# Low parts of twelve weight blocks made by accumulating transfers, in half of the value buffers

## The chip, the cores and the metric

The kernel runs on one core of a Trainium2 chip, as one program in one launch. TensorE (PE) multiplies, VectorE (DVE) and ScalarE (ACT) do elementwise work, GpSimd (POOL) has almost nothing to do here but to issue some transfers, and SyncE (SP) issues all the others. The metric is device time in microseconds (us); before the change the median of three runs is 876.96 us (876.62 to 877.98).

## The reference

One decoder layer over 512 positions of width 1024, all in float32:

```
h      = rms_norm(x)*(1+scale1)+shift1                    # scale, shift, gates: silu(c) @ w_ada
xr, gr, q, k, v, gm = split(h @ w_in)
y_rnn  = rg_lru(causal_conv(xr)) * gelu(gr)               # gated linear recurrence, 8 blocks of 128
y_attn = rms_norm(softmax(q1 k1)v - lam*softmax(q2 k2)v)  # 8 heads, two maps each, causal, rotary q, k
merged = sigmoid(gm0)*(y_rnn @ w_proj_rnn) + sigmoid(gm1)*(y_attn @ w_proj_attn)
x      = x + gate1*(merged @ w_out)
out    = x + gate2*(relu(h2 @ w_ff1)**2 @ w_ff2),  h2 = rms_norm(x)*(1+scale2)+shift2
```

## The kernel before

All large products keep float32 accuracy from a faster format: each operand is split into a high part, rounded to the matmul's format (`fp32r`), and a low part, the rest. A product is then three matmuls (`mm3`, lines 127 to 131): high by high, high by low and low by high.

Weights come in blocks of 128x1024, numbered in the order of their use (w0, w1, ...). `load_w` (lines 113 to 125) loads a block from HBM into one of three buffers (`w`, issued by SP), ScalarE rounds it to the high part `wh` (L122), and VectorE subtracts to get the low part `wl` (L123); `wh` and `wl` have two buffers each. A block feeds 24 matmuls: `project` makes one block of 128 output channels, `token_major` needs four blocks for the 512 columns of a quarter of q and k (`qk_quarter`) or of half of the values (`v_half`).

Around the change the program goes like this. After the recurrence's input and the first quarter of q and k, `v_half(0)` runs beside the recurrence's gates (`gates(n)`, n from 0 to 7): each gate takes two products of 128 channels (pg0_n, pg1_n) with small weights wgh and wgl, which live in halves (index 0 for blocks 0 to 3, index 1 for blocks 4 to 7), and ScalarE makes r, ig and th of them. Then come the attention heads, and between their steps the rest of the work is filled in by a written order, `PLAN`: gN is the gate projection gmN, sN the recurrence of block N (a product, a scan and a product on VectorE, L461, L462 and L471, and the split L473), qN a quarter of q and k, tN its transposes, v1 the second half of the values, pN the recurrence's output projection. Within that a scheduler sets the order of each engine ahead of time; each engine then works through its own list strictly in order and waits where a semaphore asks for it. A part under `tc.high_priority(n)` is drawn forward by it.

One step of a head (`softmax_step`, `weights_t`, `value_step`): TensorE makes two score banks (sc, L582), VectorE masks them and takes the maximum (L587), ScalarE makes the exponentials e (L589), VectorE joins the two maps (rr, cc and e, L593 to L596), TensorE transposes e (aT, L604), ScalarE or VectorE copies it (aTs, L607 and L609), TensorE multiplies it with the values (po, L615).

PSUM has four banks called mm (for projections), two called sc (for scores and also for pg), and single ones. The pool `v` has eight SBUF buffers of 128x512. They hold the eight halves of the gate weights (wgh, wgl), and later the four tiles of each half of the values (vs0_0 to vs0_3, vs1_0 to vs1_3), which ScalarE copies out of the mm banks (L505).

Of the kernel before, what the change touches and what calls it, by code (L numbers as in the profile page):

```python
# [17 lines left out]
F32R = mybir.dt.float32r  # L18
BF16 = mybir.dt.bfloat16
I32 = mybir.dt.int32  # L20
AF = mybir.ActivationFunctionType
ALU = mybir.AluOpType
# [18 lines left out]
QT0 = 1  # L41
ADA = (2, 4)
HP = 130
TABLES = 4
DV0, DV1 = (0,), (0,)
NWARM, NWARM2 = 2, 1
# [7 lines left out]
def build(tc, out, x, xT_in, c, pos, vecs, reps, ada, w_xr, w_xr7, w_qk, w_v, w_gr, w_gm, w_lru,  # L54
# [4 lines left out]
    with ExitStack() as es:  # L59
# [6 lines left out]
        mix_es = ExitStack()  # L66
        mix = mix_es.enter_context(tc.tile_pool(name="mix", bufs=1))

        B_Q, B_Y, B_M, B_H, B_V, B_T, B_A, B_R = 12, 24, 8, 16, 8, 4, 6, 5

        def slot(tag, bufs, name, dt=F32):
            return (big if tag in "mh" else mix).tile([P, S], dt, name=name, tag=tag, bufs=bufs)
# [35 lines left out]
        def f32(t):  # L108
            return t.bitcast(F32)

        n_unit = [0]
        last_wh = [None]

        def load_w(src, n=1024):
            u = n_unit[0]
            n_unit[0] += 1
            w = wpool.tile([P, 1024], F32, name=f"w{u}", tag="w", bufs=3)
            nc.sync.dma_start(w[:, :n], src)
            wh = wpool.tile([P, 1024], F32R, name=f"wh{u}", tag="wh", bufs=2)
            wl = wpool.tile([P, 1024], F32R, name=f"wl{u}", tag="wl", bufs=2)  # L120
            with tc.high_priority(HP):
                i_w = nc.scalar.copy(wh[:, :n], w[:, :n])  # L122
                nc.vector.tensor_tensor(wl[:, :n], w[:, :n], f32(wh)[:, :n], op=ALU.subtract)  # L123
            last_wh[0] = i_w
            return wh, wl
# [4 lines left out]
            nc.tensor.matmul(ps, lh, rl, start=False, stop=False, skip_group_check=more)  # L130
            nc.tensor.matmul(ps, ll, rh, start=False, stop=last, skip_group_check=more)  # L131

        def project(src, act, name):

            wh, wl = load_w(src)
            ps = bank(name)
            for k in range(KC):
                c0 = slice(k * P, (k + 1) * P)
                mm3(ps, wh[:, c0], wl[:, c0], act[k][0], act[k][1], k == 0, k == KC - 1)
            return ps  # L140
# [266 lines left out]
        def lru_weights():  # L407
            wg = []
            for j in range(2):
                w = wpool.tile([P, 1024], F32, name=f"wg{j}", tag="w", bufs=3)  # L410
                nc.sync.dma_start(w, w_lru[j])
                halves = []
                for i in range(2):
                    wh = slot("v", B_V, f"wgh{j}_{i}", F32R)
                    wl = slot("v", B_V, f"wgl{j}_{i}", F32R)
                    nc.scalar.copy(wh, w[:, i * S:(i + 1) * S])
                    split_l(wl, w[:, i * S:(i + 1) * S], wh)
                    halves.append((wh, wl))
                wg.append(halves)
            return wg  # L420
# [62 lines left out]
                except StopIteration as e:  # L483
                    return e.value

        def token_major(srcs, name):
            pss = [bank(f"{name}{t}") for t in range(TB)]
            for u in range(4):
                wh, wl = load_w(srcs[u])
                for t in range(TB):  # L490
                    tc0 = slice(t * P, (t + 1) * P)
                    for k2 in range(2):
                        k = 2 * u + k2
                        c0 = slice(k2 * S, (k2 + 1) * S)
                        mm3(pss[t], h[k][0][:, tc0], h[k][1][:, tc0], wh[:, c0], wl[:, c0],
                            k == 0, k == KC - 1)
                yield
            return pss

        def v_half(hf):  # L500
            pss = yield from token_major(w_v[hf], f"v{hf}_")
            vs = []
            for t in range(TB):
                v = slot("v", B_V, f"vs{hf}_{t}")
                nc.scalar.copy(v, pss[t])  # L505
                vs.append(v)
            return vs

        def qk_quarter(qt):

            pss = yield from token_major(w_qk[qt], f"qk{qt}_")
            s2 = tiny(f"qs{qt}", 32)
            rot = []
            v4 = lambda t: t.rearrange("p (m g d) -> p m g d", m=2, g=4)
# [166 lines left out]
        yr = []  # L681

        def gate(n, th):
            ps = project(w_gm[n], h, f"gm{n}")
            nc.scalar.activation(th, ps, AF.Tanh, scale=0.5)
            return th

# [450 lines left out]
```

## Time and profile before

| | |
|---|---|
| median of the runs | 876.96 us |
| the profiled execution | 876.41 us, its span 874.6 us |
| TensorE busy | 861.0 us (98%), granted clock 1.00 |
| VectorE busy | 651.5 us (74%) |
| ScalarE busy | 449.2 us (51%) |
| POOL busy | 15.1 us (2%) |
| weight blocks split by L122 and L123 | 113 |
| bytes read from HBM | 113.51 MB |

The busy time of TensorE counts a matmul from its start to its end, and matmuls overlap, so 98% doesn't say that nothing is lost; the time from the start of one matmul to the start of the next shows it. A row of the timeline gives start, duration, engine, line and operation, and in brackets how long the engine was idle before and what ended it.

### The profile page before, as it was taken

The numbers are of one execution on the slowest core, as the hardware profiler recorded it, in microseconds if no ns is written. First come the engines' busy times: TensorE is split into PE (matmuls) and PEld (weight loads), VectorE is DVE, ScalarE is ACT, GpSimd is POOL, SyncE is SP. The second block draws the span as 40 slices with busy tenths as digits, with TensorE's granted clock in tenths as the row PEclk, the third lists the DMA queues.
The fourth block names the chain that finished last, engine by engine and source line by source line (L and its number), as shares of the span: only waits on it lengthen the run. The fifth ranks groups of instructions, "written<-read, shape, count | busy, mean of one in ns | idle before, by whom it ended". The sixth has DMA issues, their size and how long they took to land.

```text
span 874.6 us, 11292 instructions
## 1 busy us (share of the span) xinstructions
PE 861.0 (98%) x4012; PEld 705.5 (81%) x4012; DVE 651.5 (74%) x1251; ACT 449.2 (51%) x748; POOL 15.1 (2%) x50
## 2 busy tenths in 40 slices
PE   6999999999999999999999999999999999999998
PEld 3888887877878888888888888888888888888887
DVE  6997995599859855786758556858766885876397
ACT  6673547985536543535623343747545544554461
POOL 1000000000000000000000000000000000002110
PEclk9999999999999999999999999999999999999999
DMA  8979425412255372238336332822641344139572
GB/s 315 370 250 319 152 97 134 136 68 73 87 131 169 99 191 76 93 87 227 110 126 210 132 121 75 273 87 72 193 148 70 128 161 169 49 126 235 120 122 96
DMA packets 64572, 128.92 MB, mean 147 GB/s; under 512 B 6146, under 2 KB 30850, under 8 KB 64516
## 3 DMA queue, kind: packets, MB, share of 16 engines
q1 hardware_dynamic: 59236, 122.97, 43.3%
q0 software_dynamic: 5280, 5.24, 3.9%
q8 instruction: 31, 0.51, 0.2%
q14 instruction: 25, 0.20, 0.1%
HBM read 113.51 MB, written 2.10 MB: 132 GB/s over the span
## 4 chain that ended last, share of the span: by engine, by line
PE 86%; DVE 10%; DMA 1%; issue 1%; ACT 1%; SPq 1%; ACTq 0%; DVEq 0%
PE f L131 6%; PE f L129 6%; PE f L130 6%; PE X L131 3%; PE X L130 3%; PE X L129 3%; PE gm L129 3%; PE gm L130 3%; PE gm L131 3%; DVE wl L123 2%; PE sc L582 2%; PE qk L131 2%; PE qk L129 2%; PE qk L130 2%; PE xr L129 2%; PE pr L129 2%
## 5 line engine op out<-in xcount | busy, mean ns | idle before, releaser
L122 ACT CAST wh<-w 128x1024 fp32r<-128x1024 f32 (+1 forms) x113 | 118.0, 1044 | 214.5 <-issue 48.1
L123 DVE TENSOR_TENSOR wl<-w,wh 128x1024 fp32r<-128x1024 f32 (+1 forms) x113 | 137.0, 1213 | 68.1 <-ACT wh L122 64.5
L131 PE MATMUL f<-h2h,wl 128*128 128x512 f32 x240 | 93.5, 390 | 0.4 <-DVE wl L123 0.4
L130 PE MATMUL f<-h2l,wh 128*128 128x512 f32 x240 | 93.2, 389 | 0.0
L129 PE MATMUL f<-h2h,wh 128*128 128x512 f32 x240 | 92.9, 390 | 0.0
L131 PEld LDWEIGHTS f<-h2h,wl 128*128 128x128 f32 x240 | 45.0, 188 | 10.1 <-DVE wl L123 0.8
L130 PEld LDWEIGHTS f<-h2l,wh 128*128 128x128 f32 x240 | 45.1, 188 | 9.4
L129 PEld LDWEIGHTS f<-h2h,wh 128*128 128x128 f32 x240 | 45.0, 188 | 9.3
L130 PE MATMUL gm<-hl,wh 128*128 128x512 f32 x128 | 51.0, 398 | 0.0
L129 PE MATMUL qk<-wh,hh 128*128 128x512 f32 x128 | 50.7, 396 | 0.0
L129 PE MATMUL gm<-hh,wh 128*128 128x512 f32 x128 | 50.5, 394 | 0.0
L131 PE MATMUL gm<-hh,wl 128*128 128x512 f32 x128 | 50.5, 394 | 0.0
L131 PE MATMUL qk<-wh,hl 128*128 128x512 f32 x128 | 50.4, 394 | 0.0
L130 PE MATMUL qk<-wl,hh 128*128 128x512 f32 x128 | 50.4, 394 | 0.0
L941 DVE TENSOR_TENSOR p_1l<-b,p_1h 128x1024 fp32r<-128x1024 f32 x24 | 29.4, 1223 | 26.3 <-ACT p_1h L940 26.1
L589 ACT ACTIVATE e<-e,nm 128x128 f32<-128x128 f32 (+3 forms) x64 | 35.7, 559 | 24.4 <-DVE nm L587 24.4
L940 ACT CAST p_1h<-b 128x1024 fp32r<-128x1024 f32 x24 | 25.2, 1051 | 31.0 <-PE f L130 22.9
L941 DVE TENSOR_TENSOR p_0l<-b,p_0h 128x1024 fp32r<-128x1024 f32 x24 | 29.3, 1223 | 15.0 <-ACT p_0h L940 13.8
L587 DVE CUSTOM_DVE_ANT_0 e<-sc,mask 128x128 f32<-128x128 f32 (+3 forms) x64 | 30.3, 484 | 9.9 <-PE sc L582 9.9
L940 ACT CAST p_0h<-b 128x1024 fp32r<-128x1024 f32 x24 | 25.3, 1055 | 24.2 <-PE X L131 12.4
L188 DVE CUSTOM_DVE_ANT_0 ada<-ada,cb,bada 128x1024 f32<-128x1024 f32 x16 | 20.5, 1283 | 14.3 <-DMA ada<-in_ada 14.1
L984 DVE TENSOR_TENSOR b<-b,b 128x1024 f32<-128x1024 f32 x24 | 29.1, 1220 | 0.1
(444 smaller groups left out, 2216.9 us busy)
## 6 DMA issues: line engine op xcount, KB each, us to landing
ada<-in_ada SPq DMA_DIRECT2D x64, 256.0 KB, 5.8
w<-in_w_ff SPq DMA_DIRECT2D x32, 512.0 KB, 3.2
b<-in_w_ff SPq DMA_DIRECT2D x30, 512.0 KB, 3.4
w<-in_w_qk SPq DMA_DIRECT2D x16, 512.0 KB, 3.2
w<-in_w_gm SPq DMA_DIRECT2D x16, 512.0 KB, 3.7
ada<-in_ada SPq DMA_DIRECT2D x16, 512.0 KB, 3.3
b_t<-in_w_ff POOLq DMA_DIRECT2D x10, 512.0 KB, 6.5
w<-in_w_gr SPq DMA_DIRECT2D x8, 512.0 KB, 4.0
```

Source lines behind the costliest of these rows:

```text
L122: i_w = nc.scalar.copy(wh[:, :n], w[:, :n])
L123: nc.vector.tensor_tensor(wl[:, :n], w[:, :n], f32(wh)[:, :n], op=ALU.subtract)
L129: nc.tensor.matmul(ps, lh, rh, start=first, stop=False, skip_group_check=more)
L130: nc.tensor.matmul(ps, lh, rl, start=False, stop=False, skip_group_check=more)
L131: nc.tensor.matmul(ps, ll, rh, start=False, stop=last, skip_group_check=more)
L188: nc.vector.tensor_tensor_reduce(w, w, cb, 1.0, bada[:, col:col + 1], op0=ALU.mult, op1=ALU.add, accum_out=mod[:, col:col + 1])
L582: nc.tensor.matmul(ps[m][:, :nn], q[m][:, qc], k[m][r][:, :nn], start=r == 0, stop=r == 1)
L587: nc.vector.tensor_tensor_reduce(e[:, :n], ps[m][:, :n], mask[:, S - n:], 1.0, 1e30, op0=ALU.add, op1=ALU.min, accum_out=nm)
L589: nc.scalar.activation(e[:, :n], e[:, :n], AF.Exp, bias=nm, scale=-1.0, accum_out=sums[:, m:m + 1])
L940: nc.scalar.copy(v4(wh), v)
L941: nc.vector.tensor_tensor(v4(wl), v, f32(v4(wh)), op=ALU.subtract)
L984: nc.vector.tensor_tensor(d, d, s_, op=ALU.add)
```

## The change

`load_w` gets a second way, `by_dma`, for twelve blocks: the gate projections gm2 to gm5 (blocks w27, w28, w33, w34) and the second and third quarter of q and k (w29 to w32, w35 to w38). There ScalarE writes, for each half of the block, the negated and rounded weight into a buffer, and GpSimd issues a transfer that reads the same half of the weight from HBM once more and adds it to the buffer: weight minus its high part. VectorE's subtraction falls away. The buffers for it are four of the eight `v` buffers, now called `u`; the other four stay `v`. The gate weights' halves with index 0 live in `u`, those with index 1 in `v`; the first half of the values is in `v`, the second in `u`. The negated copy is drawn forward by 260, the rounding copy by 130 as before. `Pair` lets the two halves be addressed as one tile.

```diff
+HP_DMA = 260
+DMA_G, DMA_Q = (2, 3, 4, 5), (1, 2)
-        B_Q, B_Y, B_M, B_H, B_V, B_T, B_A, B_R = 12, 24, 8, 16, 8, 4, 6, 5
+        B_Q, B_Y, B_M, B_H, B_V, B_T, B_A, B_R = 12, 24, 8, 16, 4, 4, 6, 5
...
+            if by_dma:
+                lows = []
+                with tc.high_priority(HP_DMA):
+                    for i in range(2):
+                        cols = slice(i * S, (i + 1) * S)
+                        wl = slot("u", B_V, f"wl{u}_{i}", F32R)
+                        nc.scalar.activation(wl, w[:, cols], AF.Copy, scale=-1.0)
+                        nc.gpsimd.dma_start(wl, src[:, cols].bitcast(F32R), accum_op=ALU.add)
+                        lows.append(wl)
+                wh = wpool.tile([P, 1024], F32R, name=f"wh{u}", tag="wh", bufs=2)
+                with tc.high_priority(HP):
+                    last_wh[0] = nc.scalar.copy(wh, w)
+                return wh, Pair(lows)
...
-                    wh = slot("v", B_V, f"wgh{j}_{i}", F32R)
-                    wl = slot("v", B_V, f"wgl{j}_{i}", F32R)
+                    wh = slot("v" if i else "u", B_V, f"wgh{j}_{i}", F32R)
+                    wl = slot("v" if i else "u", B_V, f"wgl{j}_{i}", F32R)
...
-                v = slot("v", B_V, f"vs{hf}_{t}")
+                v = slot("u" if hf else "v", B_V, f"vs{hf}_{t}")
...
-            pss = yield from token_major(w_qk[qt], f"qk{qt}_")
+            pss = yield from token_major(w_qk[qt], f"qk{qt}_", qt in DMA_Q)
...
-            ps = project(w_gm[n], h, f"gm{n}")
+            ps = project(w_gm[n], h, f"gm{n}", n in DMA_G)
```

The scheduler orders all engines anew with this. ScalarE at the end of the recurrence's gates, before (the last number of a name counts the buffers; pg0_7 and pg1_7 are the last gate's products, v0_0 to v0_3 the banks of the values' first half):

```order
L505 COPY vs0_0_1725<-v0_0_1349 128x512
L436 CAST xch7_1706<-xc7_1337 128x512
L505 COPY vs0_1_1727<-v0_1_1350 128x512
L505 COPY vs0_2_1729<-v0_2_1351 128x512
L122 CAST wh26_1872<-w26_1870 128x1024
L444 ACTIVATE r6_1699<-pg0_6_1691,vec_93 128x512
L446 ACTIVATE ig6_1701<-pg1_6_1692,vec_93 128x512
L449 ACTIVATE th6_1704<-r6_1699,sp4_624 128x512
L444 ACTIVATE r7_1718<-pg0_7_1710,vec_93 128x512
L446 ACTIVATE ig7_1720<-pg1_7_1711,vec_93 128x512
L449 ACTIVATE th7_1723<-r7_1718,sp4_624 128x512
L505 COPY vs0_3_1731<-v0_3_1352 128x512
```

And ScalarE at the same place now:

```order
L148 CAST wh26_1872<-w26_1870 128x1024
L470 ACTIVATE r6_1699<-pg0_6_1691,vec_93 128x512
L472 ACTIVATE ig6_1701<-pg1_6_1692,vec_93 128x512
L475 ACTIVATE th6_1704<-r6_1699,sp4_624 128x512
L138 ACTIVATE wl27_0_1905<-w27_1903 128x512
L138 ACTIVATE wl27_1_1908<-w27_1903 128x512
L470 ACTIVATE r7_1718<-pg0_7_1710,vec_93 128x512
L138 ACTIVATE wl28_0_1970<-w28_1968 128x512
L138 ACTIVATE wl28_1_1973<-w28_1968 128x512
L472 ACTIVATE ig7_1720<-pg1_7_1711,vec_93 128x512
L475 ACTIVATE th7_1723<-r7_1718,sp4_624 128x512
L531 COPY vs0_0_1725<-v0_0_1349 128x512
```

Three copies of the values (vs0_0 to vs0_2) moved from ahead of the gates' last functions to behind them, and four negated copies (wl27, wl28) came in between.

TensorE at the same place, before (gm0 is the first gate projection, sc0_0_0 and sc0_0_1 the score banks of head 0's first step):

```order
L129 MATMUL gm0_1776<-hh0_195,wh25_1772 128x512
L130 MATMUL gm0_1776<-hl0_199,wh25_1772 128x512
L129 MATMUL pg0_7_1710<-xch7_1706,wgh0_1_760 128x512
L130 MATMUL pg0_7_1710<-xcl7_1708,wgh0_1_760 128x512
L131 MATMUL pg0_7_1710<-xch7_1706,wgl0_1_761 128x512
L129 MATMUL pg1_7_1711<-xch7_1706,wgh1_1_770 128x512
L130 MATMUL pg1_7_1711<-xcl7_1708,wgh1_1_770 128x512
L131 MATMUL pg1_7_1711<-xch7_1706,wgl1_1_771 128x512
L131 MATMUL gm0_1776<-hh0_195,wl25_1773 128x512
L129 MATMUL gm0_1776<-hh1_238,wh25_1772 128x512
L582 MATMUL sc0_0_0_1751<-kh0_2_0_1473,qs0_0_0_1458 128x256
L582 MATMUL sc0_0_0_1751<-kl0_2_0_1476,qs0_0_0_1458 128x256
```

And TensorE now, from the last gate's second product on (sc0_1_0 and sc0_1_1 are the banks of head 0's second step):

```order
L155 MATMUL pg1_7_1711<-xch7_1706,wgh1_1_770 128x512
L156 MATMUL pg1_7_1711<-xcl7_1708,wgh1_1_770 128x512
L157 MATMUL pg1_7_1711<-xch7_1706,wgl1_1_771 128x512
L608 MATMUL sc0_0_0_1751<-kh0_2_0_1473,qs0_0_0_1458 128x256
L608 MATMUL sc0_0_0_1751<-kl0_2_0_1476,qs0_0_0_1458 128x256
L608 MATMUL sc0_0_1_1752<-kh0_2_1_1479,qs0_0_1_1461 128x256
L608 MATMUL sc0_0_1_1752<-kl0_2_1_1482,qs0_0_1_1461 128x256
L608 MATMUL sc0_1_0_1804<-kh0_2_0_1473,qs0_0_0_1458 128x256
L608 MATMUL sc0_1_0_1804<-kl0_2_0_1476,qs0_0_0_1458 128x256
L608 MATMUL sc0_1_1_1805<-kh0_2_1_1479,qs0_0_1_1461 128x256
L608 MATMUL sc0_1_1_1805<-kl0_2_1_1482,qs0_0_1_1461 128x256
L155 MATMUL gm0_1776<-hh0_195,wh25_1772 128x512
```

Before, gm0 had started ahead of the last gate and the scores stood among its matmuls; now the whole of gm0 follows the scores of two steps.

VectorE between the masking of head 0's second step and the product that joins its maps (e0_1_0, L596 before and L622 now), before:

```order
L609 COPY aTs0_0_1824<-aT0_0_1822 128x128
L461 SCALAR_TENSOR_TENSOR xc0_1050<-r0_1395,xc0_1050 128x512
L123 TENSOR_TENSOR wl28_1967<-w28_1964,wh28_1966 128x1024
L593 RECIPROCAL rr0_1749<-sm0_1_1803 128x2
L462 SCALAR_TENSOR_TENSOR xc0_1050<-r0_1395,xc0_1050 128x512
L595 SCALAR_TENSOR_TENSOR cc0_1_1819<-sm0_1_1803,nlam_633,rr0_1749 128x1
L471 TENSOR_TENSOR xc0_1050<-xc0_1050,gel0_1048 128x512
L596 SCALAR_TENSOR_TENSOR e0_1_0_1811<-e0_1_1_1815,cc0_1_1819,e0_1_0_1811 128x256
```

And now (the rows of L488 are the scans):

```order
L487 SCALAR_TENSOR_TENSOR xc0_1050<-r0_1395,xc0_1050 128x512
L635 COPY aTs0_0_1824<-aT0_0_1822 128x128
L488 SCALAR_TENSOR_TENSOR xc0_1050<-r0_1395,xc0_1050 128x512
L497 TENSOR_TENSOR xc0_1050<-xc0_1050,gel0_1048 128x512
L619 RECIPROCAL rr0_1749<-sm0_1_1803 128x2
L487 SCALAR_TENSOR_TENSOR xc1_1088<-r1_1442,xc1_1088 128x512
L621 SCALAR_TENSOR_TENSOR cc0_1_1819<-sm0_1_1803,nlam_633,rr0_1749 128x1
L488 SCALAR_TENSOR_TENSOR xc1_1088<-r1_1442,xc1_1088 128x512
L622 SCALAR_TENSOR_TENSOR e0_1_0_1811<-e0_1_1_1815,cc0_1_1819,e0_1_0_1811 128x256
```

The subtraction for block 28 is gone, and the first two steps of the next recurrence (xc1) stand ahead of the product.

## Rows read from the trace of the kernel before

**Rows 1.** The page, head.
```profile
span 874.6 us, 11292 instructions
```
**Rows 2.** Busy time by stretch: stretch, length, engines with instructions, clock, transfer engines, GB/s.
```profile
600.00:650.00 50.00, 50.00 (x223) 41.39 (x222) 35.73 (x39) 26.61 (x35) 0.00 (x0) 1.00 0.46 154
150.00:250.00 100.00, 97.41 (x463) 78.50 (x462) 82.86 (x188) 65.50 (x130) 0.00 (x0) 1.00 0.30 93
```
**Rows 3.** TensorE's waits, 150 to 250 us: for whom, us, times, longest.
```profile
PE aT L604 <- DVE e L596: 1.5, 4, 0.7
PE qT L547 <- DVE raw L535: 0.7, 1, 0.7
PE yT L642 <- DVE o L635: 0.4, 1, 0.4
```
**Rows 4.** Timeline of TensorE, 163 to 172 us: start, duration, instruction.
```profile
164.04 0.50 PE L129 MATMUL pg<-xch,wgh 128*128 128x512 f32 x1
...
165.31 0.39 PE L131 MATMUL pg<-xch,wgl 128*128 128x512 f32 x1
...
171.62 0.40 PE L129 MATMUL gm<-hh,wh 128*128 128x512 f32 x1
```
**Rows 5.** Timeline of ScalarE, 159 to 168 us.
```profile
159.07 0.59 ACT L505 COPY vs<-v 128x512 f32<-128x512 f32 x1
...
163.31 0.68 ACT L444 ACTIVATE r<-pg,vec 128x512 f32<-128x512 f32 x1
...
164.46 0.72 ACT L449 ACTIVATE th<-r,sp 128x512 f32<-128x512 f32 x1
165.07 0.69 ACT L444 ACTIVATE r<-pg,vec 128x512 f32<-128x512 f32 x1
165.73 0.69 ACT L446 ACTIVATE ig<-pg,vec 128x512 f32<-128x512 f32 x1
166.32 0.71 ACT L449 ACTIVATE th<-r,sp 128x512 f32<-128x512 f32 x1
166.93 0.58 ACT L505 COPY vs<-v 128x512 f32<-128x512 f32 x1
167.51 1.28 ACT L453 ACT_TABLE_LOAD   x1
```
**Rows 6.** Groups by line and shape: busy us, mean ns, idle before.
```profile
L123 DVE TENSOR_TENSOR wl<-w,wh 128x1024 fp32r<-128x1024 f32 x105 | 128.3, 1222 | 67.7 <-ACT wh L122 64.1 <-DMA kl<-ql 2.9 <-DMA kh<-qh 0.2
...
L436 ACT CAST xch<-xc 128x512 fp32r<-128x512 f32 x8 | 4.8, 618 | 0.0
...
L256 ACT ACTIVATE x<-x,rs 128x512 f32<-128x512 f32 x3 | 1.9, 713 | 0.0
```
**Rows 7.** Timeline of VectorE, 178 to 182 us.
```profile
178.83 1.22 DVE L123 TENSOR_TENSOR wl<-w,wh 128x1024 fp32r<-128x1024 f32 x1
179.97 0.16 DVE L593 RECIPROCAL rr<-sm 128x2 f32<-128x2 f32 x1
180.04 1.20 DVE L462 TENSOR_TENSOR_SCAN xc<-r,xc 128x512 f32<-128x512 f32 x1
...
181.89 0.48 DVE L596 SCALAR_TENSOR_TENSOR e<-e,cc,e 128x256 f32<-128x256 f32 x1
```
**Rows 8.** Timeline of TensorE, two of its waits.
```profile
182.42 0.44 PE L604 MATMUL aT<-ident,e 128*128 128x128 f32 x2 [0.19 <-DVE e L596]
...
246.60 0.30 PE L547 MATMUL qT<-ident,raw 128*128 128x128 f32 x1 [0.74 <-DVE raw L535]
```
**Rows 9.** Transfers (KB each, us from issue to landing), and POOL's issue beside VectorE.
```profile
xo<-in_xT_in SPq DMA_DIRECT2D x8, 256.0 KB, 2.9
...
b_t<-in_w_ff POOLq DMA_DIRECT2D x10, 512.0 KB, 6.5
...
841.37 1.27 POOL L917 DMA_DIRECT2D b_t<-in_w_ff  x1 [1.87 <-DVE p_0l L941]
841.59 1.22 DVE L143 TENSOR_TENSOR s4l<-sx,s4h 128x1024 fp32r<-128x1024 f32 x1
```

More of the change, by code (lines that the diff above doesn't have):

```diff
@@ L109, in f32, with __init__, __getitem__, load_w @@
             return t.bitcast(F32)
+        class Pair:
+            def __init__(self, tiles):
+                self.tiles = tiles
+            def __getitem__(self, where):
+                rows, cols = where
+                i = cols.start // S
+                return self.tiles[i][rows, cols.start - i * S:cols.stop - i * S]
         n_unit = [0]
         last_wh = [None]
-        def load_w(src, n=1024):
+        def load_w(src, n=1024, by_dma=False):
             u = n_unit[0]
@@ L131, in mm3, with project @@
             nc.tensor.matmul(ps, ll, rh, start=False, stop=last, skip_group_check=more)
-        def project(src, act, name):
-            wh, wl = load_w(src)
+        def project(src, act, name, by_dma=False):
+            wh, wl = load_w(src, by_dma=by_dma)
             ps = bank(name)
@@ L484, in run, with token_major @@
                     return e.value
-        def token_major(srcs, name):
+        def token_major(srcs, name, by_dma=False):
             pss = [bank(f"{name}{t}") for t in range(TB)]
             for u in range(4):
-                wh, wl = load_w(srcs[u])
+                wh, wl = load_w(srcs[u], by_dma=by_dma)
                 for t in range(TB):
```

## The prediction

> **What bounds the kernel now.** I read the page's totals first, then the busy time of each engine in stretches, then TensorE's own waits, then the order of single instructions where the change begins. The profiled execution took 876.41 us for a span of 874.6 us [rows 1], so 1.8 us lie around the span; the median of the runs shown is 876.96 us. In a stretch where nothing disturbs it, TensorE is busy all the time and runs 223 matmuls in 50 us, 0.224 us for one of 512 columns [rows 2]; a block of weights is 24 of them, 5.4 us. A matmul is drawn 0.39 us long because they overlap, so a wait of TensorE is about 0.16 us longer than the idle time that the profile gives. Between 150 and 250 us, where eleven of the twelve changed blocks lie, VectorE is busy for 82.86 of 100 us, ScalarE for 65.50, and TensorE lacks 2.59 us [rows 2]. The waits named there are six: four for a softmax product (L596), one for the turned queries (L535), one for a head's normed output (L635), 2.6 us together [rows 3], and with 0.16 us each some 3.6 us. All six are VectorE. That is all that a lighter VectorE can win in this stretch; after 320 us the order of the instructions is the same before and after, so nothing is won there.
>
> **The change part by part.** Twelve subtractions of 1.222 us leave VectorE [rows 6]; they start 1.14 us apart from the next instruction, so 12 x 1.14 = 13.7 us. Twenty-four negated copies of 128x512 come onto ScalarE. No row shows one; the nearest are the rounding copy of the same size from the same memory, 0.618 us, and a scaled copy, 0.713 us [rows 6]. ScalarE's next instruction starts up to 0.10 us before the end of the one before it (r, 0.69 us long, starts 0.66 us before ig; ig, 0.69 long, 0.59 before th [rows 5]), so one costs 0.52 to 0.61 us of its queue; I take 0.52, since the scale is a constant. In sum 12.5 us.
>
> *The first place: the end of the recurrence gates.* The value buffers shrink from eight to four, and all four now hold gate weights of blocks 4 to 7, so the first copy of the values, vs0_0, which ran at 159.07 us before [rows 5], can run only after the last gate's matmuls (pg0_7, pg1_7). The gate projection gm0 takes its PSUM bank from vs0_0. So gm0 can no longer stand beside the gates and the first scores, and the order puts the eight score matmuls of head 0 ahead of all of it. They need banks that ScalarE frees by r7 and ig7, and ScalarE's order now has two negated copies ahead of r7 and two between r7 and ig7. By rows: pg0_7 starts at 164.04, when r6 (163.31 plus 0.68 us) has freed its bank, and the last of pg1_7 at 165.31 [rows 4, 5]; this stays. ScalarE is through with th6 at 165.07 [rows 5]. Then two negated copies (1.04), r7 (0.66) from 166.11, two more (1.04), ig7 (0.59) from 167.81, th7 (0.61) from 168.40, vs0_0 from 169.01 with 0.58 us: it ends at 169.6. The scores fit in meanwhile. gm0 starts at about 169.6, and gm1 24 matmuls later, at 175.0. Before, gm1 started at 171.62 [rows 4] with the same work behind it. This costs 3.4 us. The other three vs copies follow, then the table load that stood at 167.51 [rows 5]: 169.6 plus 3 x 0.48 is 171.1, so ScalarE, and VectorE which waits for its square roots, are late by 3.5 us too. Nobody gains on TensorE by the delay. Bounds: with 0.61 us a copy 3.8; if the copies cost nothing in the queue, vs0_0 would still be behind th7 and end at 167.5, and gm1 would start at 172.9, 1.3 us late.
>
> *The second place: the softmax of head 0 and 1.* The freed time on VectorE does not come to the products for which TensorE waits. Before, the third copy's subtraction (178.83) stood between two rows of head 0's softmax, and the product followed at 181.89 [rows 7]. In the new order the subtraction is gone, but the next block's recurrence (one product of 0.6 us and a scan of 1.12 us) stands there: minus 1.14, plus 1.72, so the product comes some 0.6 us later counted from its scores, and TensorE, which waited for it until 182.42 [rows 8], waits on. I worked the next three in the same way (scores, recurrence steps, product) and find the waits before the third and fourth transposes and before head 0's output still there, within 0.5 us of what they were. Behind head 1 the recurrences are done early, and the last two waits shrink: the one for the turned queries, 0.74 us idle at 246.60 [rows 8], by about half, since its chain loses three subtractions but now stands behind a negated copy that waits for the end of a projection. I take 0.8 us won; bounds are 3.6 won and 1 lost.
>
> *The accumulating transfers.* A new block's low part is there only when its buffer is free (two blocks back), the copy is made, the transfer issued on POOL, and landed. No row shows such a transfer of 256 KB. Plain ones of 256 KB land in 2.9 us, accumulating ones of 512 KB in 6.5 us [rows 9]; I take 5.0, nearer to the latter, which is of the same kind and queue. While attention stands between the blocks, one turn is well over 6 us and hides it. In the four blocks of the third quarter it is 5.4 us: the second half has its copy at 1.04 us, its issue some 1.6 us after the first's, and lands near 7.3 us, where TensorE wants it at 5.4 + 0.9 = 6.3. Two of the four blocks have both halves freed that late; transposes of the queries take up part of it. I take 0.8 us; bounds 0 (2.9 us to landing) and 6 (6.5 us and every late block exposed).
> In the trace an issue on POOL took 1.27 us (841.37 to 842.64) with a subtraction of VectorE (841.59 to 842.81) beside nearly all of it [rows 9]. The Trainium skill (SBUF — State Buffer, section "SBUF: two separate sides") warns that a transfer issued from GpSimd starves while VectorE runs a copy in a mode that takes the port both share. A subtraction is no such copy, and the row shows that it holds nothing back; no row shows an issue beside a copy of VectorE, of which there are a few here, so the rule would act as rival (b) below does.
>
> *Smaller.* Copies of transposed softmax weights on ScalarE (aTs1_1) now stand behind a weight copy that waits for the end of a block: 0 to 0.6 us, I take 0.3. Reading weights twice adds 12 x 0.5 MB to transfer engines that are a third busy here: nothing. The order at 55 to 75 us moves a little, with no wait of TensorE near: nothing.
>
> Sum: 3.4 - 0.8 + 0.8 + 0.3 = 3.7 us. The profiled execution would be 876.4 + 3.7 = 880.1, and the median 876.96 + 3.7, about 880.7.
>
> **The rivals.** (a) *VectorE's relief pays back the delay.* Place: the six waits of the stretch; if all go, 3.6 us come back, and the sum is 3.4 - 3.6: 876.8 us, not slower. It decides if the forecast's second place is wrong: VectorE must reach each product at least as early as TensorE, by then 3.4 us late, asks for its transpose. For it: VectorE does lose 13.7 us of work in a stretch where it ends every wait. Against it: the recurrence steps pulled forward fill the same time until head 1 is through. With a shorter first delay (1.3 us, the lower bound) it would even be 874.7. (b) *The transfers land late.* Place: blocks 35 to 38. At 6.5 us to landing and with each late half exposed, 3.4 - 0.8 + 6 + 0.3 = 8.9: 885.9 us. For it: the 6.5 us and the order, which gives the copy no start before the block two back has ended; against it: half the bytes. (c) *ScalarE becomes the bound.* Its load in these 100 us goes from 65.5 to some 78, and a copy that waits for a buffer holds up the exponentials behind it. If three of the eight rounds of heads 0 and 1 are held for 1 us each, it is 3.7 + 3 = 6.7: 883.7 us. For it: two copies stand between exponentials of one pair; against: by the walk their buffers are free within about 1 us of their turn.
>
> **How the numbers follow.** Forecast 0.50, (a) 0.22, (b) 0.16, (c) 0.12. The range takes the forecast's own (879 to 883), most of (c) and (b), and half of (a): 877.4 to 885.0. A difference under 0.2%, 1.75 us, can't be told from none. Forecast, (b) and (c) are slower by more; of (a), 0.06 is faster by more (with the smaller first delay) and 0.16 within. So faster 0.06, same 0.16, slower 0.78.
>
> **What would show it.** In the profile after: idle of TensorE before the score matmuls and before gm0 between 165 and 170 us, released by ScalarE's r, ig and vs, some 3 us by start to start; gm1's first matmul near 175.0; the table load near 171; the softmax waits (L622 in the new file) still there until about 215 us, and little of them behind; landing of the wl transfers of 4 to 5.5 us. The forecast is wrong if gm1 starts before 173.5, if those softmax waits are gone, or if TensorE idles for a POOL transfer by more than 2 us in all.

## The result and the profile after

The changed kernel takes 885.95 us (median of 5 runs, 885.05 to 887.84), the kernel before 877.11 us in the same session (5 runs, 876.62 to 877.98). The ratio is 1.0102, with a 95% interval of 1.0088 to 1.0117: 8.8 us slower, where 3.7 had been forecast, and outside the range. The sign was right, the size was not, and it falls on the price of rival (b). In the rows of the changed kernel every line number of the program is 26 higher than in the rows of before (L596 is L622, L604 is L630, and so on); the experiments shift the numbers by a few lines more, and there the names tell which operation is meant.

Two lines of the page of the changed kernel: the span, and the granted clock in 40 slices.

```profile
span 885.9 us, 11364 instructions
...
PEclk9999999899999999999999999999999999999999
```

This answers [rows 1]. The profiled execution is the longest of the five, 11.3 us over the span of before. The prediction had no term for the one 8 in the clock line. The next two answers are the busy time by stretch, as in [rows 2], of the changed kernel: first TensorE alone by 5 us about the end of the gates, then all engines by 25 us.

```profile
165.00:170.00 5.00, 3.11 (x12) 0.81 0.74 172
170.00:175.00 5.00, 5.00 (x13) 0.50 0.84 143
```

```profile
150.00:175.00 25.00, 22.74 (x86) 17.42 (x85) 11.06 (x19) 19.94 (x34) 3.67 (x4) 0.86 0.79 181
...
225.00:250.00 25.00, 23.51 (x108) 19.23 (x107) 16.26 (x48) 15.52 (x33) 6.22 (x9) 1.00 0.80 168
250.00:275.00 25.00, 22.29 (x107) 16.96 (x106) 8.20 (x21) 11.20 (x23) 2.71 (x4) 1.00 0.83 188
```

The second number is TensorE's busy time, the last three are clock, busy share of the transfer engines and GB/s. VectorE (the third engine, 11.06 us in the first of these rows) is indeed lighter: before, it was busy for 14.28 us there. TensorE loses most in the first and the last of these stretches; the transfer engines are busy for about 0.8 of the time in all three. TensorE's waits between 130 and 340 us are, in the order of their sums:

```profile
PE qk L156 <- DMA wl<-in_w_qk: 2.5, 2, 1.5
PE sc L608 <- DMA kh<-qh: 1.3, 1, 1.3
PE sc L608 <- ACT r L470: 1.1, 1, 1.1
PE yT L668 <- DVE o L661: 0.8, 1, 0.8
PE aT L630 <- DVE o L656: 0.7, 1, 0.7
PE aT L630 <- DVE e L622: 0.7, 2, 0.5
```

Against [rows 3], the two longest are new and are transfers: low parts that have not landed, and keys that have not been moved. To see when, add up by how much each matmul starts later than the usual distance behind one of the size before it (the median of that size in the trace, 0.227 us for 512 columns). By stretches of 25 us from 150 us on this gives, before and after: 0.6 and 6.6, 3.1 and 2.2, 1.8 and 2.9, 1.4 and 2.0, 1.4 and 4.9 us. From 275 us to the end the two differ by 1.1 us.

**The first place.** TensorE in the changed kernel at the end of the gates, then ScalarE:

```profile
165.30 0.40 PE L157 MATMUL pg<-xch,wgl 128*128 128x512 f32 x1
166.84 0.38 PE L608 MATMUL sc<-kh,qs 128*128 128x256 f32 x1 [1.14 <-ACT r L470]
...
169.98 0.63 PE L155 MATMUL gm<-hh,wh 128*128 128x512 f32 x1
170.41 0.63 PE L156 MATMUL gm<-hl,wh 128*128 128x512 f32 x1
...
175.04 0.40 PE L155 MATMUL gm<-hh,wh 128*128 128x512 f32 x1
...
177.77 0.39 PE L155 MATMUL gm<-hh,wh 128*128 128x512 f32 x1
```

```profile
165.06 1.15 ACT L138 ACTIVATE wl<-w 128x512 fp32r<-128x512 f32 x2
166.10 0.68 ACT L470 ACTIVATE r<-pg,vec 128x512 f32<-128x512 f32 x1
166.67 1.15 ACT L138 ACTIVATE wl<-w 128x512 fp32r<-128x512 f32 x2
167.71 0.69 ACT L472 ACTIVATE ig<-pg,vec 128x512 f32<-128x512 f32 x1
...
168.89 2.05 ACT L531 COPY vs<-v 128x512 f32<-128x512 f32 x4
```

Held against [rows 4, 5], the walk through ScalarE's queue was right to 0.12 us in each step: r7 at 166.10 (forecast 166.11), ig7 at 167.71 (167.81), vs0_0 at 168.89 (169.01). gm0 starts at 169.98 (169.6). But its first twelve matmuls start 0.427 us apart, not 0.227: the granted clock is 0.50 between 170 and 175 us, the lower of TensorE's two levels, 1.2 instead of 2.4 GHz, after a stretch in which TensorE was busy for 3.11 of 5 us. 12 x 0.2 is 2.4 us. So gm1 starts at 177.77, not at 175.0.

**The last four blocks** (35 to 38, the query and key quarter). Transfers between 220 and 265 us, KB each and median us from issue to landing, first of the changed kernel, then of the kernel before:

```profile
wl<-in_w_qk POOLq DMA_DIRECT2D x8, 256.0 KB, 5.8
w<-in_w_qk SPq DMA_DIRECT2D x3, 512.0 KB, 6.2
w<-in_w_v SPq DMA_DIRECT2D x3, 512.0 KB, 6.5
...
kh<-qh SPq DMA_DIRECT2D x4, 128.0 KB, 5.3
```

```profile
w<-in_w_qk SPq DMA_DIRECT2D x3, 512.0 KB, 3.2
w<-in_w_v SPq DMA_DIRECT2D x3, 512.0 KB, 3.3
kh<-qh SPq DMA_DIRECT2D x6, 128.0 KB, 2.7
```

The transfers that both kernels have take about twice as long. The 24 accumulating ones land in 3.6 to 8.1 us, in the answer for their tile:

```profile
DMA to landing us min/median/max: 3.6/5.4/8.1
```

The two for which TensorE waits are second halves: block 35's, issued at 238.2 and landed 6.1 us later, and block 37's, issued at 250.0 and landed after 7.6 us. The first half of block 37 had gone out 0.7 us earlier on the same queue and landed in 3.6 us, as the answer for these two says, and then TensorE's waits:

```profile
L139 POOL DMA_DIRECT2D wl<-in_w_qk x2: 841/942/1042, 249.3 to 250.0; - x2
...
DMA to landing us min/median/max: 3.6/5.6/7.6
```

```profile
244.37 0.50 PE L156 MATMUL qk<-wl,hh 128*128 128x512 f32 x1 [1.49 <-DMA wl<-in_w_qk]
...
257.59 0.50 PE L156 MATMUL qk<-wl,hh 128*128 128x512 f32 x1 [1.03 <-DMA wl<-in_w_qk]
...
263.56 0.35 PE L608 MATMUL sc<-kh,qs 128*128 128x256 f32 x1 [1.25 <-DMA kh<-qh]
```

Start to start these are 1.65, 1.19 and 1.42 us over the usual distance. Of the 24 accumulating transfers the six that were issued with no other of them under way landed in 3.6 to 4.7 us; those issued behind one that had not landed took up to 8.1 us.

### The profile page after: what moved, and what is told of

It reads as the page before. It is cut to its first block, busy times and chain, and to the rows that moved or that the text cites. A ratio compares the mean times of both kernels' runs of the same rounds, so it can differ in the third digit from the quotient of the medians.

```text
span 885.9 us, 11364 instructions
## 1 busy us (share of the span) xinstructions
PE 865.5 (98%) x4012; PEld 707.8 (80%) x4012; DVE 638.7 (72%) x1239; ACT 461.5 (52%) x772; POOL 35.7 (4%) x74
## 4 chain that ended last, share of the span: by engine, by line
PE 74%; issue 10%; DMA 7%; DVE 6%; POOL 1%; ACT 1%; SPq 1%; POOLq 0%; DVEq 0%; ACTq 0%
PE f L157 6%; PE f L155 6%; PE f L156 6%; PE X L157 3%; PE X L155 3%; PE X L156 3%; DMA ada<-in_ada 3%; PE sc L608 2%; DVE wl L149 2%; PE gm L155 2%; PE gm L156 2%; PE gm L157 2%; PE pr L156 2%; PE pr L155 2%; PE pr L157 2%
## 5 line engine op out<-in xcount | busy, mean ns | idle before, releaser
L148 ACT CAST wh<-w 128x1024 fp32r<-128x1024 f32 (+1 forms) x101 | 105.4, 1043 | 211.2 <-issue 50.5
L149 DVE TENSOR_TENSOR wl<-w,wh 128x1024 fp32r<-128x1024 f32 (+1 forms) x101 | 122.3, 1211 | 70.4 <-ACT wh L148 69.6
L922 POOL DMA_DIRECT2D b_t<-in_w_ff x8 | 10.2, 1274 | 582.8 <-DVE p_1l L967 543.7
L156 PEld LDWEIGHTS qk<-wl,hh 128*128 128x128 f32 x128 | 24.1, 188 | 7.8 <-DMA wl<-in_w_qk 3.4
```

The source lines that it names most:

```text
L922: nc.gpsimd.dma_start(b, src_b(*p_, hf), accum_op=ALU.add)
```

## The experiments

Three theories stood at the start. A: the first place (buffers, ScalarE's queue, and the clock behind it) makes the loss. C: the transfers make it, in the last four blocks, either because their own low part is late (C2) or because they slow the others (C1). D: VectorE's relief is real and only covered. Ratios are to the kernel before, with 95% intervals, and times are medians; one us is 0.00114.

**split_only: the divided buffers alone.**

```
-DMA_G, DMA_Q = (2, 3, 4, 5), (1, 2)
+DMA_G, DMA_Q = (), ()
```

> The value buffers stay divided in two sets of four as in the changed kernel, but no low part is made by a transfer (both lists of blocks are empty); the twelve subtractions are back on VectorE. Theory A (the 8.8 us are mainly the first place, and most of that is the queue of negated copies on ScalarE): vs0_0 still waits for the last gate, but has no copies ahead of it, so it ends near 167.5 us and the first gm projection starts about 1.3 us late: 877.1 + 1.3 = 878.4 us, granted clock 1.00 throughout. Theory B (the division of the buffers alone is what costs): gm0 starts near 169.8 us as in the changed kernel, TensorE's clock falls behind it, and the time is 877.1 + 3.8 + 1.5 to 2.6 = 882.4 to 883.5 us. Theory C (the cost is the transfers and comes later in the kernel): 877.1 to 878.4 us, no tell from A by itself.

878.84 us, 1.0015 (1.0006 to 1.0024), clock 1.00. The divided buffers cost 1.3 us, as the lower bound of the first place said. That fits A and also C, whose upper figure is the same; B is out.

**gm_only and qk_only: transfers for four or for eight blocks.**

```
+DMA_G, DMA_Q = (2, 3, 4, 5), ()      # gm_only
+DMA_G, DMA_Q = (), (1, 2)            # qk_only
```

> The changed kernel with transfers for the four gm blocks alone; the eight blocks of the query and key quarters get their low parts from VectorE again. Theory A: the first place is the same as in the changed kernel, gm0 starts near 169.8 us, the clock falls: 877.1 + 3.8 + 1.5 = 882.4 us (to 883.5 where the clock falls in full). Theory C: the waits at 242 to 262 us go, so at most 877.1 + 3.8 + clock as well, but TensorE shows no wait for a low part or a key. If the first place were a small part and the later one large: 879 us.

> The changed kernel with transfers for the eight blocks of the two query and key quarters alone; the gm blocks get their low parts from VectorE. Theory A: no negated copies stand ahead of vs0_0, so the first place costs 1.3 us and the clock stays at 1.00; the later waits stay. Sum with theory C's 2.8 us for low parts and 1.4 us for keys: 877.1 + 1.3 + 4.2 = 882.6 us. If the later waits in the changed kernel follow only from its lateness at the first place: 878.4 us.

gm_only: 881.49 us, 1.0046 (1.0033 to 1.0059), no wait for a low part or a key. The first place costs some 4 us. Its profile has the same stall of TensorE and a clock of 1.00; three of its five runs have 0.997 or 0.998: the stall does not always bring the lower clock. qk_only: 886.12 us, 1.0102 (1.0085 to 1.0120), 3.5 us more than expected. Without most of the first place it is as slow as the changed kernel, so A cannot be the whole. In its profile TensorE waits 2.5 us for a turned query from VectorE and 2.1 us for keys, and the clock is 0.94 and 0.93 in the two stretches of 25 us from 225 us on, where these waits lie.

**wl_pool: all transfers, no first place.**

```
-                        wl = slot("u", B_V, f"wl{u}_{i}", F32R)
+                wl = wpool.tile([P, 1024], F32R, name=f"wl{u}", tag="wl", bufs=2)
...
-                    wh = slot("v" if i else "u", B_V, f"wgh{j}_{i}", F32R)
+                    wh = slot("v", B_V, f"wgh{j}_{i}", F32R)
```

> The same twelve blocks get their low parts by negated copies and accumulating transfers, but in the two buffers wl that the subtraction used before (two halves of one 128x1024 tile); the eight value buffers are as before, so vs0_0 and gm0 are not held back. Theory A (first place and clock): 885.95 less 3.8 for gm1's delay and less 1.5 for the clock leaves 880.6 us or less, gm1 starts near 171.6 us, clock 1.00. Theory C (transfers): the waits for the low parts in the third quarter (2.8 us by start to start) and for the keys' transfer (1.4 us) remain, so 877.1 + 4.2 = 881.3 us; both together say 880 to 881.5. Rival D (VectorE's relief is real and was only hidden by the first place): below 877.1, about 875.5 us, with the waits for the softmax products gone.

885.22 us, 1.0094 (1.0078 to 1.0109): all theories missed, by 4 us and more. gm0 and gm1 stand as before (gm1 at 171.79), the clock is 1.00 in the profile (0.995 to 0.998 in the other three runs), and the time is still that of the changed kernel. TensorE's waits in it:

```profile
PE qk L154 <- DMA wl<-in_w_qk: 3.7, 5, 1.9
PE gm L155 <- DMA wl<-in_w_gm: 1.2, 1, 1.2
PE sc L606 <- DMA kh<-qh: 1.0, 1, 1.0
```

What TensorE no longer loses at the first place it loses waiting for transfers. The buffers differ too, so by itself this does not say that the same transfers would cost 8 us in the changed kernel's buffers; qk_only, which has those, says the same: 8.9 us with eight blocks, where gm_only has 4.0 with the other four. The costs do not add.

**no_transfer and wl_copies: the copies without the transfers.**

```
-                        nc.gpsimd.dma_start(wl, src[:, cols].bitcast(F32R), accum_op=ALU.add)
```

(The line was taken out of the changed kernel, and out of wl_pool.)

> The changed kernel with its 24 negated copies, but without the 24 accumulating transfers: the low part is left as the negated high part, so the output is not the reference's. Everything else, the buffers and the order on ScalarE included, stays. Theory A+C (first place 3.8 us plus what the clock loses, then transfers 4.2 us): 877.7 + 3.8 to 5.3 = 881.5 to 883 us, with no waits of TensorE between 225 and 265 us beyond those of the kernel before. Theory C alone decides the later waits: TensorE must show none for keys either. Rival E (ScalarE, where a negated copy that waits for its buffer holds up what stands behind it): the later waits stay, 885 to 886 us.

> The kernel with low parts in the wl buffers and undivided value buffers (885.2 us), without its 24 transfers: the negated copies alone, 12.5 us more on ScalarE and 13.7 us less on VectorE; the low part is left as the negated high part, so the output is not the reference's. If ScalarE carries them at no cost: 877.9 us, as with VectorE's relief alone. Rival (c) of the prediction (ScalarE becomes the bound): 880 us or more, with TensorE waiting for softmax products behind held exponentials.

no_transfer: 881.03 us, 1.0042 (1.0030 to 1.0054); TensorE waits for no key, and the keys' transfers land in 2.4 us. wl_copies: 877.06 us, 0.9999 (0.9990 to 1.0007). Theory C stands: taking out the transfers wins 4.9 us in the changed kernel, and 8.2 us in the one without the first place. Rival (c) and E fall: 24 copies more on ScalarE cost nothing outside the first place. The clock falls at the first place in no_transfer too (0.84 and 0.82 in the two stretches of 5 us from 165 us on), so the transfers are not needed for that.

**relief: VectorE's relief alone.**

```
-                lows = []
-                with tc.high_priority(HP_DMA):
...
-                return wh, Pair(lows)
+                return wh, wh
...
-                v = slot("u" if hf else "v", B_V, f"vs{hf}_{t}")
+                v = slot("v", B_V, f"vs{hf}_{t}")
```

(against the changed kernel; the whole making of the low part is out, and the value buffers are eight again, so it differs from the kernel before by the twelve subtractions alone)

> The kernel before with the subtraction of the twelve blocks left out and nothing in its place: the high part is used where the low part belongs, so the output is not the reference's. No negated copies, no transfers, eight value buffers. It prices VectorE's relief alone, 12 x 1.14 us. Rival (a) of the prediction (all six waits of TensorE between 180 and 247 us are VectorE's and go): 877.5 - 3.6 = 873.9 us. If the recurrence steps that follow take the freed time, as the prediction's walk had it for head 0 and part of head 1: 877.5 - 0.8 = 876.7 us.

877.87 us, 1.0011 (1.0003 to 1.0020): nothing is won. Of the waits in its profile,

```profile
PE aT L622 <- DVE e L614: 1.3, 3, 0.8
PE yT L660 <- DVE o L653: 1.1, 1, 1.1
PE qT L565 <- DVE raw L553: 0.9, 1, 0.9
```

all kinds of [rows 3] are still there, 3.3 us together against 2.6. So they do not come from these twelve subtractions; that they are the length of chains is my reading, which no run shows. D and rival (a) fall.

**shadow: the transfers, with nobody waiting for them.**

```
+                        nc.gpsimd.tensor_copy(jk[:, :1], w[:, i:i + 1])
+                        nc.gpsimd.dma_start(jk, src[:, cols], accum_op=ALU.add)
```

(added to split_only, into four buffers that are idle there)

> The kernel with the divided value buffers and no low part made by a transfer (878.84 us when it was measured), with 24 accumulating transfers of the same weights added that nobody waits for: they go into four spare buffers, each after a 128x1 copy on GpSimd that ties it to its block's weights. VectorE keeps its subtractions and ScalarE has no negated copies. Theory C1 (the transfers take bandwidth from the others, and the keys' and queries' transfers come late for that): 878.8 + 1.4 to 4 = 880.2 to 882.8 us, with TensorE waiting for keys or for transposed queries near 245 to 262 us, and landings of the keys' transfers near 5 us instead of 2.7. Theory C2 (only the matmuls that wait for a late low part cost): 878.8 us, no new waits.

879.05 us, 1.0018 (1.0009 to 1.0027), 0.2 us over split_only. Its landings between 225 and 265 us:

```profile
junk<-in_w_qk POOLq DMA_DIRECT2D x6, 256.0 KB, 5.8
...
kh<-qh SPq DMA_DIRECT2D x6, 128.0 KB, 3.0
```

The same bytes on the same queue, just as slow to land, cost nothing here, as C2 has it. But these transfers wait for no buffer: the last is issued near 240 us, eleven before the first of the queries', so C1 was not tested at the place where the keys move. With the late keys of the changed kernel beside it, neither C1 nor C2 is the whole, and it seems to matter when the transfers run.

**depth4 and depth4_last: buffers free earlier.**

```
+                if u % 2:
+                    wt = wpool.tile([P, 1024], F32R, name=f"wl{u}", tag="wl", bufs=2)
...
+                        wl = wt[:, cols] if u % 2 else slot("u", B_V, f"wl{u}_{i}", F32R)
```

(wt is a wl buffer of the pair that stands idle; depth4_last does it from block 35 on)

> The changed kernel, but every other of the twelve blocks takes its low part in the pair of wl buffers that stands idle in this stretch, so a buffer is free four blocks back instead of two and the negated copies and transfers can start earlier. Theory C2 (a turn of two blocks is too short for the landing): the waits for low parts at 242 and 256 us go, 885.95 - 2.8 = 883.1 us. Theory C1 (bandwidth): the transfers bunch up, the waits move to the keys' transfers, 885 to 887 us. The first place stays as it is in both.

> As the kernel with low parts in the wl buffers for every other block, but only from block 35 on: blocks 35 and 37 use the pair of wl buffers, 36 and 38 the four value buffers, all before them as in the changed kernel. Theory C (in the last four blocks a buffer comes free too late for copy, issue and landing, and the late transfers then meet the keys'): both waits for low parts and the keys' wait go, 885.95 - 4.2 = 881.7 us, the keys' transfers land in 2.4 to 3 us. If the negated copies pulled forward hold up ScalarE as they did near 199 us where all blocks used both sets: 883 to 885 us.

886.32 us, 1.0095 (1.0078 to 1.0113), and 887.15 us, 1.0111 (1.0094 to 1.0127). In the profile of depth4 what C2 said of the last four blocks comes true: no wait for a low part or a key there, keys land in 2.4 us, and TensorE loses 2.6 us between 225 and 275 us, as before (2.8), instead of 6.9. Two new waits eat it, and the clock falls at other places (0.83 from 180 to 190 us and from 200 to 210 us). TensorE's two waits, then ScalarE's rows behind the longer one:

```profile
PE aT L632 <- DVE e L624: 3.5, 1, 3.5
PE gm L159 <- DMA wl<-in_w_gm: 1.9, 1, 1.9
```

```profile
199.58 0.63 ACT L140 ACTIVATE wl<-w 128x512 fp32r<-128x512 f32 x1 [3.30 <-DMA w<-in_w_qk]
200.12 0.71 ACT L617 ACTIVATE e<-e,nm 128x512 f32<-128x512 f32 x1
```

The negated copy, now free of its buffer, goes far forward in ScalarE's queue and waits there for its weights, with head 0's exponentials behind it. In depth4_last such a copy waits 1.9 us for its weights near 222 us, a gm block's negated copies stand behind it, and TensorE waits 1.9 us for that block's low part. The cost moved, and was not paid off.

**wl_gm and gm_q1: fewer blocks.**

```
+DMA_G, DMA_Q = (2, 3, 4, 5), ()      # wl_gm: in wl_pool
+DMA_G, DMA_Q = (2, 3, 4, 5), (1,)    # gm_q1: in the changed kernel
```

> Transfers for the four gm blocks alone, in the wl buffers that the subtraction used, with the eight value buffers undivided: neither the first place nor the query and key blocks. If the four transfers are hidden: 877.7 us. With the wait for the first of them that the kernel with all twelve in these buffers showed (1.4 us by start to start at 177.5 us): 879.1 us. If VectorE's relief by four subtractions pays: 876.5 us.

> The changed kernel without the transfers of the last four of the twelve blocks (the quarter that is projected at 238 to 262 us, blocks 35 to 38); the four gm blocks and the first query and key quarter keep them. If what comes after the first place is lost in those last four blocks alone: the time of the kernel with transfers for gm only, 881.5 us (877.5 + 3.8 to 4). If the first quarter costs as much: 883.5 us.

wl_gm: 878.56 us, 1.0016 (1.0007 to 1.0025), with the wait of 1.3 us for the first low part. gm_q1: 883.76 us, 1.0073 (1.0060 to 1.0085): halfway. No low part is waited for, but the lost time in its profile is spread (clock 0.93 from 150 to 175 us, a key 0.6 us late). Why the first quarter costs some 2 us beyond gm_only is not settled.

**hp130: the negated copies later in ScalarE's queue.**

```
-HP_DMA = 260
+HP_DMA = 130
```

> The changed kernel with the priority of the negated copies and their transfers at 130 instead of 260, that of the rounding copies. In ScalarE's order two negated copies instead of four then stand ahead of vs0_0, and none ahead of r7. If each copy ahead costs its 0.52 to 0.57 us at the first place: vs0_0 ends near 168.4 us instead of 169.5, TensorE stalls 1.1 us less, so 885.95 - 1.1 = 884.9 us, and less again if the clock keeps to 1.00. Against it stand negated copies made later: if the landings are what costs behind the first place, they get later too, and the time is 885.5 to 888 us with longer waits for low parts.

885.0 us, 1.0086 (1.0073 to 1.0100): the number of the first expectation, but the interval reaches into that of the changed kernel (1.0088 to 1.0117), so the gain of 1 us is not clear of noise. In its profile TensorE loses 3.1 us between 150 and 175 us instead of 6.6 (the clock, now 1.00, is about 2.4 of the difference), and waits 2.9 us for low parts instead of 2.5: most of the 3.5 us is not seen in the time.

**plain: the transfers without the addition.**

```
-                        nc.gpsimd.dma_start(wl, src[:, cols].bitcast(F32R), accum_op=ALU.add)
+                        nc.gpsimd.dma_start(wl, src[:, cols].bitcast(F32R))
```

> The changed kernel, but the 24 transfers copy the weights into the low part's buffer instead of adding them, so the output is not the reference's; copies, buffers, queue and waits are the same. If the addition is what makes them slow: they land in about 3 us as the plain transfers of 256 KB in the kernel before, the waits for low parts and keys between 240 and 262 us go, 885.95 - 4.2 = 881.7 us. If any transfer issued there is late (the turn of buffers, the copy and the issue take the time): landings of 4 to 5 us, waits shorter by half, 884 us; if nothing changes, 886 us.

884.25 us, 1.0080 (1.0067 to 1.0093): by its time the middle case. Landings between 225 and 265 us:

```profile
wl<-in_w_qk POOLq DMA_DIRECT2D x8, 256.0 KB, 3.8
...
kh<-qh SPq DMA_DIRECT2D x4, 128.0 KB, 4.7
```

The waits for low parts are gone, but the keys and queries are still slow: TensorE waits 1.6 us for a transposed query whose buffer a queries' transfer still holds (VectorE waits 5.2 us for it). So about 3.2 us (884.25 - 881.03) come with any transfer at this place and 1.7 us with the addition; the second figure is only just clear of noise, since the intervals of the two kernels touch. The two halves of block 37, 0.7 us apart here too, land in 3.0 and 3.7 us; with the addition it was 3.6 and 7.6.

**keepwarm: no lower clock.**

```
+            if n == KC - 1:
+                pw = bank("pw", "tp", 1)
+                for _ in range(14):
+                    nc.tensor.matmul(pw, h[0][0][:, :P], h[0][0], start=True, stop=True)
```

> The changed kernel with 14 matmuls of 512 columns into an unused bank of TensorE's output memory, two ahead of the last gate's matmuls and twelve behind, where TensorE otherwise stands still between 165.5 and 169.8 us; nobody reads them. 14 x 0.227 = 3.2 us, all of it in the stall. If the clock falls for that stall: the granted clock between 165 and 175 us is 1.00, gm0's matmuls start 0.227 us apart, and the time is 885.95 less 1.0 to 1.5 us of the clock, about 884.7 us. If the fall has another cause: still 886 us, with gm0 at half speed.

```profile
165.00:170.00 5.00, 4.57 (x24) 3.71 (x23) 1.63 (x6) 5.00 (x10) 3.67 (x4) 1.00 0.69 163
170.00:175.00 5.00, 5.00 (x25) 4.13 (x24) 1.85 (x4) 4.98 (x9) 0.00 (x0) 1.00 0.91 154
```

In the profile the clock stays at 1.00, gm0 starts at 169.97 and runs at full speed, and gm1 starts at 175.65, so the stall brought the fall there. Two of the four runs have a mean clock of 0.998 and 0.997 all the same; where it fell in them, no trace shows. And the kernel takes 886.73 us, 1.0107 (1.0094 to 1.0120), not 884.7: in its profile TensorE waits 1.8 us for a key, and 2.2 us for low parts. The 2.4 us were lost again at the transfers.

## Why the prediction was wrong

- **The first place: right, 3.4 forecast.** With TensorE at full clock (keepwarm) gm1 comes at 175.65, 4.0 us later than before, and the table load at 170.95 (171 forecast). Its parts show as experiments: 1.3 us for the divided buffers (split_only), 3.7 us with the copies in ScalarE's queue (no_transfer, which has all edits but the transfers; the same terms made 3.4 - 0.8 + 0.3 = 2.9 us).
- **The softmax waits: -0.8 forecast, nothing found.** That VectorE's relief would not reach the products was the right reason; relief shows that it holds everywhere, the later waits too. Rival (a), given 0.22, has no base: all kinds of wait outlive the removal of the twelve subtractions, so these did not make them. Its price was also short: 3.4 - 3.6 leaves out the 0.8 and 0.3 us of the other terms, with which it is 877.9 us, not 876.8.
- **The accumulating transfers: 0.8 forecast, 4.9 measured** (885.95 less no_transfer's 881.03; 5.3 by the two ratios). This is the step that failed, and the prediction's own sign of it came: TensorE idles 2.5 us for low parts, where more than 2 us was to show it wrong. The bounds, 0 and 6, held; the value taken between them did not. Three parts of the working were off. The landing was taken as 5.0 us for each half, as if neither held up the other; the median was 5.4, but the two landings that mattered took 6.1 and 7.6 us, both second halves issued while an earlier transfer of the kind was still under way. The exposure was reckoned as 1.0 us in two blocks, partly covered; it was 2.8 us start to start. And "Reading weights twice adds 12 x 0.5 MB to transfer engines that are a third busy here: nothing" used a mean of 100 us. Where the low parts of the last four blocks are fetched, the stretch from 225 to 250 us was quiet before (0.25), and with the added transfers the engines are busy for 0.80 of it; from 250 to 275 us the engines were busy for 0.82 already, as the next rows, of the kernel before, show, and there the keys' transfers went from 2.7 to 5.3 us. The keys had no term at all.

```profile
225.00:250.00 25.00, 24.26 (x109) 19.48 (x109) 22.47 (x55) 10.43 (x21) 0.00 (x0) 1.00 0.25 84
250.00:275.00 25.00, 25.00 (x130) 20.45 (x129) 16.48 (x43) 13.74 (x30) 0.00 (x0) 1.00 0.82 211
```

- **The clock: no term.** It fell to its lower level in the stall that the prediction itself had foreseen. In the profile it takes 2.4 us of TensorE's time; among the five runs the one with a clock of 1.00 took 885.05 us, the two with 0.996 took 886.96 and 887.84. But keepwarm was no faster than the median, in the two runs with a clock of 1.00 (886.18 and 886.75 us) either. What the clock costs in the end is open.
- **The sum.** The prediction added places as if each moved the end by its own price. The runs show two delays side by side: without the first place the loss is 8.2 us (wl_pool, in other buffers), without the transfers 3.7 (no_transfer), with both 8.9. What TensorE gains early it waits for at the transfers. I read this as the transfers' own chain (buffer free two blocks back, copy behind what stands in ScalarE's queue, issue, landing) setting the end, with the first place hidden behind it; each edit also makes a new order of all engines, and no run separates the two. Rival (b) named the place. That its price, 885.9 us, is the time measured is luck: it is made of 6 us for late low parts and 0.8 us won on the softmax waits, and the runs show 2.8 us for low parts, late keys that it did not name, and nothing won.
- **Rival (c)** was wrong: 24 copies of 0.63 us cost nothing (wl_copies), except where they stand ahead of vs0_0, and where one of them waits in the queue ahead of exponentials (depth4).

What stays open is the spread cost of the first quarter's transfers (gm_q1), and how much of the keys' lateness belongs to the accumulating transfers and how much to the value weights loaded at the same time; no_transfer says only that without the former both are quick. Open too is why the parts do not add up: that the transfers' chain hides the first place is argued, not shown.

## What to carry to other kernels

Before a transfer takes over work of an engine, read the busy share of the transfer engines in the very stretch where it will run, and list what else must land there; a landing time read in quiet does not hold, and two such transfers issued close together did not land side by side here. Relief of a busy engine is worth something only if the waits that it ends come from its load: a run with the work simply left out tells that at once. And where an edit delays an engine at one place and a chain at another, do not add the two: ask which of them would set the end if the other were gone.

## What the runs showed of the hardware

- An accumulating transfer of 256 KB from GpSimd's queue took 5.8 us to land between 220 and 265 us (the median of eight), a plain one in the same place 3.8 us (plain). With none other of the kind under way it was 3.6 to 4.7 us, and 7.6 us for one issued 0.7 us behind another. In the changed kernel the accumulating kind occupied 46.0% of the 16 engines' time in these 45 us for 3.42 MB, the ordinary queue 36.1% for 4.66 MB: 1.7 times as much per byte. Against plain transfers on the same queue (plain, 27.9% of the 40 us from 225 us on for 3.03 MB) it is 1.6 times. The rows, first of the changed kernel, then of plain:

```profile
q0 software_dynamic: 1877, 3.42, 46.0%
q1 hardware_dynamic: 1633, 4.66, 36.1%
```

```profile
q0 software_dynamic: 1671, 3.03, 27.9%
```

- TensorE's granted clock was 0.81 in a stretch in which it was busy for 3.11 of 5 us, and 0.50 in the 5 us behind it; with 14 matmuls that nobody reads in the stall it stayed at 1.00 in the profile. The same stall (a wait of 1.1 to 1.2 us for r, and TensorE busy for 2.8 to 3.1 us between 165 and 170 us) stands in the profiles of six kernels; the clock fell between 165 and 175 us in five of them (the changed kernel, no_transfer, plain, gm_q1, depth4_last) and not in gm_only. In qk_only (0.94 and 0.93 in the two stretches of 25 us from 225 us on) and in depth4 (0.83 from 180 to 190 us) it fell at other places.
- The Trainium skill (SBUF — State Buffer, section "SBUF: two separate sides") says that GpSimd cannot write the descriptors of a transfer that it issues while VectorE runs an operation in a mode that takes the port both share. The changed kernel shows no issue held up so: issues with work of VectorE beside them took 0.84 to 1.54 us (the longest began while another issue was still under way), those with none 0.84 to 1.05 us, and the one beside a copy of VectorE (L635, at 196 us) 0.84 us. The two issues behind TensorE's waits took 0.85 and 1.04 us, and the landings 6.1 and 7.6.
